# Nine groups of the down projection: each product of 264 token columns sent as two of 132

## The chip, the cores and the metric

The kernel runs on one core of a Trainium2 chip. The metric is the device time of one execution in microseconds; two executions of the kernel before took 1300.14 and 1300.42 us, median 1300.28. The core has TensorE (matrix products), VectorE, ScalarE, GpSimd, and SyncE, which here only issues DMA transfers. In the profile PE is TensorE's stream of products and PEld its stream of weight loads.

## The reference

One inference step of a decoder layer over 256 prompt tokens and 8 single-token samples, 264 token columns in all, with a model width of 2048 and an inner width of 8192. Cut to the part that the change touches:

```python
hid = jnp.square(jax.nn.relu(rms_norm(x, g_mlp) @ w_up))   # (264, 8192)
x = x + hid @ w_down                                       # (264, 2048)
...
y_prompt = rms_norm(xp, g_final)
```

Ahead of it stand an input projection, three gated branches (pooling, a linear recurrence, a convolution) and an output projection. All data are 32-bit floats.

## The kernel before

**Layout.** Features lie on the 128 partitions and the 264 tokens along the free axis, so a product is a 128 x 128 block of weights (stationary) times 128 x 264 activations (moving) into an accumulator of 128 x 264 in one of eight PSUM banks.

**Three products per block.** For precision each operand is split into a high part, rounded to the type that TensorE takes in one pass (float32r), and the low rest. `mm3` (line 183) sends for one block `whi x xh`, `whi x xl` and `wlo x xh`, lines 185, 186 and 187, all into the same accumulator. `sent` (line 165) orders the moving columns: column 2j is token j and column 2j + 1 is token j + 132; `res` (line 172) reads the accumulator back in the order of the tokens.

**Stream of weights.** `weight_plan` (line 57) lists groups; a group makes four output tiles (512 output features) from k-tiles of 128 rows. All groups are cut into chunks of 1024 weights a partition (two k-tiles by 512 columns). SyncE's queue brings two chunks with one transfer, ScalarE rounds a chunk to `whi` (line 162), VectorE subtracts to `wlo` (line 163), each three chunks ahead of TensorE, in four buffers.

**The loop.** The loop over `chunks` (line 916) is the order of all engines, written out by hand. For a chunk of a group, `tile_mm` (line 901) is called for 2 k-tiles x 4 output tiles. With the last chunk of a group its four accumulators are evacuated, and the next group goes on in the other four banks.

**The MLP.** It runs in four quarters q of the inner width: four groups `w_up`, then four groups `w_down` (m = 0 to 3, 16 k-tiles from k0 = 16 q). The activations of a quarter are in `A` (q even) or in `LH` and `Q` (q odd), by `hid` (line 798). `down_evac` (line 824) adds an accumulator to the residual `X` (line 830); in the fourth quarter it also starts the final norm, whose sums are products with a constant tile `ones` (line 980). The down projection has 16 groups of 8 chunks; a group has 8 x 2 x 4 x 3 = 192 products.

```python
mm3(pss[m], whi[:, i % NHI, s], wlo[:, i % NHI, s], xh, xl, c == 0 and kt == 0 and gi > 2, stop)
```

Of the kernel before, what the change touches and what calls it, by code (L numbers as in the profile page):

```python
# [13 lines left out]
ALU = mybir.AluOpType  # L14
# [6 lines left out]
N = TP + TS  # L21
# [26 lines left out]
NHI = 4  # L48
# [8 lines left out]
def weight_plan():  # L57

    groups = [("w_lru_in", 0, 2 * WIDE, 0)] + [("w_in", WIDE, KD - WIDE, m) for m in (1, 2)]
    groups += [("w_in", 0, 16, m) for m in (0, 3, 4, 6, 5)]
    for g in range(4):
        groups += [("w_gate", 0, 16, t) for t in ((0, 4, 1), (5,), (2, 6), (3, 7))[g]]
        groups += [("w_pool_br", 0, 4, g), ("w_lru_br", 0, 8, g)]
    groups += [("w_gate", 0, 16, 8 + g) for g in range(3)]
    groups += [("w_conf_br", 0, 4, 0), ("w_gate", 0, 16, 11)]
    groups += [("w_conf_br", 0, 4, g) for g in range(1, 4)]
    groups += [("w_out", 0, 16, m) for m in range(4)]
    for q in range(4):  # L70
        groups += [("w_up", 0, 16, q * 4 + m) for m in range(4)]
        groups += [("w_down", q * 16, 16, m) for m in range(4)]
    chunks = []
    for gi, (name, _, k, m) in enumerate(groups):
        for c in range(k // 2):
            chunks.append(("wide" if name == "w_lru_in" else "dense", gi, c, CH))
            if name == "w_in" and (m, c) in LRU_AT:
                chunks.append(("lru", LRU_AT.index((m, c)), 0, 512))
            if (name, m) == ("w_gate", 0) and c == 3:
                chunks += [("grp", 0, 0, 512), ("none", 0, 0, 0)]  # L80
    return groups, chunks
# [3 lines left out]
def hybrid_step(ctx: ExitStack, tc: tile.TileContext, head_in, x_in, par_in, st_in, wall, y_out, st_out):  # L85
    nc = tc.nc
# [9 lines left out]
    whi = cpool.tile([P, NHI, CH], F32R, name="whi")  # L96
    wlo = cpool.tile([P, NHI, CH], F32R, name="wlo")
    qtmp = cpool.tile([P, 16 * N], F32, name="qtmp", tag="Q")
    first = cpool.tile([P, KD + EARLY * ROW], F32, name="first")
    early = first[:, KD:].rearrange("p (k c) -> p k c", k=EARLY)  # L100
    X = cpool.tile([P, KD, N], F32, name="X")
# [19 lines left out]
    def acc():  # L121
        return psum.tile([P, 512], F32, name="acc", tag="acc")
# [7 lines left out]
    groups, chunks = weight_plan()  # L130
# [34 lines left out]
    def sent(x):  # L165

        return x.rearrange("p (t j) -> p j t", t=2)

    def halves(x):
        return x.rearrange("p (t j) -> p t j", t=2)  # L170

    def res(ps):

        return ps[:, :N].rearrange("p (j t) -> p t j", t=2)

    def spread(prompt, sample, ps, f):

        r, h = res(ps), N // 2
        for d, a, t in ((prompt[:, :h], r[:, 0, :], slice(0, h)), (prompt[:, h:], r[:, 1, :TP - h], slice(h, TP)),
                        (sample, r[:, 1, TP - h:], slice(TP, N))):  # L180
            nc.vector.tensor_tensor(d, a, f[:, t], op=ALU.mult)

    def mm3(ps, whi_t, wlo_t, xh, xl, first, last):
        xh, xl = sent(xh), sent(xl)
        nc.tensor.matmul(ps[:, :N], whi_t, xh, start=first, stop=False)  # L185
        nc.tensor.matmul(ps[:, :N], whi_t, xl, start=False, stop=False)  # L186
        nc.tensor.matmul(ps[:, :N], wlo_t, xh, start=False, stop=last)  # L187
# [19 lines left out]
    def later(n, fn):  # L207
        delayed.append((now[0] + n, fn))
# [26 lines left out]
    def spend(**kw):  # L235
        for e, c in kw.items():
            credit[e] -= c
# [133 lines left out]
    TM, GEL, RA, _ = B  # L371
# [22 lines left out]
    def lru_x_evac(ct, ps):  # L394
        spread(el[:, ct, 3:], st_lc[:, ct, :, 3], ps, rstd)
        spend(dve=0.5)
# [165 lines left out]
    def ca_evac(ct, ps):  # L562
        spread(vext[:, ct, 30:], st_cc[:, ct, :, 30], ps, SG[:, ct, :])
        spend(dve=0.5)
# [89 lines left out]
    def pool_evac(gi, ps):  # L654
        spread(pext[:, gi, 15:], st_po[:, gi, :, 15], ps, rstd)
        spend(dve=0.5)
# [135 lines left out]
    def square_add(m, add=True):  # L792
        t = sq2 if m == 0 else G[:, 21 + m % 3, :]
        nc.scalar.activation(t, X[:, m, :], AF.Square)  # L794
        if m and add:
            nc.gpsimd.tensor_tensor(sq2, sq2, t, op=ALU.add)  # L796
# [24 lines left out]
    def half(h):  # L821
        return slice(h * (N // 2), (h + 1) * (N // 2))

    def down_evac(q, m, ps):
        if (q, m) == (3, KD - 1):
            for h in range(2):
                nc.vector.tensor_tensor(X[:, m, half(h)], X[:, m, half(h)], res(ps)[:, h, :], op=ALU.add)
                nc.vector.tensor_tensor(G[:, 11, half(h)], X[:, m, half(h)], X[:, m, half(h)], op=ALU.mult)
            return
        nc.vector.tensor_tensor(halves(X[:, m, :]), halves(X[:, m, :]), res(ps), op=ALU.add)  # L830
        spend(dve=0.4)
        if q == 3:
            def rest():
                square_add(m, m < KD - 2)
                nc.scalar.activation(X[:, m, :], X[:, m, :], AF.Copy, scale=gfin[:, m:m + 1])

            later(0 if m >= KD - 4 else 1 + m % 4 // 2, rest)


    def group(gi):  # L840
        name, k0, _, m = groups[gi]
        if name == "w_in":
            def rhs(i):
                return A[:, i, :], A[:, 16 + i, :]
            fn = {0: pool_evac, 1: lru_x_copy, 2: lambda c, p: lru_x_evac(4 + c, p), 3: gel_evac,
                  4: lambda c, p: gel_evac(4 + c, p), 5: ca_evac, 6: cb_evac}[m]
            return rhs, fn
        if name == "w_gate":
            return (lambda i: (A[:, i, :], A[:, 16 + i, :])), (lambda c, p: gate_evac(m // 4, m % 4, c, p))
        if name == "w_pool_br":  # L850
            assert "grp" in done
            return (lambda i: (Q(i), Q(8 + i))), (lambda c, p: branch_evac(0, m, c, p))
        if name == "w_lru_br":
            assert "lru" in done
            return (lambda i: (LH(i), LH(8 + i))), (lambda c, p: branch_evac(1, m, c, p))
        if name == "w_conf_br":
            assert "conf" in done
            return (lambda i: (Q(4 + i), Q(12 + i))), (lambda c, p: branch_evac(2, m, c, p))
        if name == "w_out":
            return (lambda i: (A[:, i, :], A[:, 16 + i, :])), (lambda c, p: out_evac(m * 4 + c, p))  # L860
        if name == "w_up":
            return bpart, (lambda c, p: up_evac(m // 4, (m % 4) * 4 + c, p))
        q = k0 // 16
        return (lambda i: hid(q, i)), (lambda c, p: down_evac(q, m * 4 + c, p))
# [36 lines left out]
    def tile_mm(i, gi, c, kt, m, rhs, pss, stop):  # L901
        s = slice(kt * 512 + m * P, kt * 512 + (m + 1) * P)
        xh, xl = rhs(2 * c + kt + (WIDE if gi < 3 else 0))
        mm3(pss[m], whi[:, i % NHI, s], wlo[:, i % NHI, s], xh, xl, c == 0 and kt == 0 and gi > 2, stop)


# [8 lines left out]
    pss = None  # L915
    for i, ch in enumerate(chunks):
# [17 lines left out]
        kind, gi, c, _ = ch  # L934
        if kind == "dense":
            rhs, fn = group(gi)
            n = groups[gi][2] // 2
            if c == 0:
                pss = [acc() for _ in range(4)] if gi > 2 else pair[4 * gi - 4:4 * gi]
            if i < len(chunks) - 2:  # L940
                for kt in range(2):
                    if i == 13 and kt == 1:
                        x_rms()
                    for m in range(4):
                        tile_mm(i, gi, c, kt, m, rhs, pss, c == n - 1 and kt == 1)
            elif i == len(chunks) - 1:
                for m in range(4):
                    for b in range(4):
                        tile_mm(i - 1 + b // 2, gi, c - 1 + b // 2, b % 2, m, rhs, pss, b == 3)
            if c == n - 1:  # L950
                for m in range(4):
                    fn(m, pss[m])
                after(gi)
        elif kind == "lru":
            for j in range(2):
                lru_gate_mm(2 * gi + j, i, j)
            if gi == 3:
                lru_tail()
        elif kind == "grp":
            grp_mm(i)  # L960
# [16 lines left out]
    ps = [acc(), acc()]  # L977
# [4 lines left out]
    t, last = G[:, 9, :], acc()  # L982
# [129 lines left out]
```

## Time and profile before

| | |
|---|---|
| two executions | 1300.14, 1300.42 us (median 1300.28) |
| span of the profiled execution, first to last instruction | 1299.3 us |
| mean granted TensorE clock | 0.997 |
| products, weight loads | 11434, 11434 |
| moved from and to memory | 252.03 MB read, 3.21 MB written, 196 GB/s over the span |
| last product of the down projection | starts at 1287.0 us |

The profile gives an instruction's line in the kernel, its engine, output and inputs by the program's names, and its time from the span's start. A product's record is longer than the step from one product to the next, since products are pipelined. Idle time before an instruction is put down to what released it. A line such as 187 belongs to a helper; the tiles tell which stage called it (`A` or `LH` and `Q` as the moving side are the activations of the down projection, among others).

### The profile page before, as it was taken

The page shows a single profiled execution, that of the slowest core. Times are in us where ns is not written, and L with a number is a line of the kernel's source. Part 1 is how long each engine was busy: PE and PEld are TensorE (multiplying, and loading weights), DVE is VectorE, ACT ScalarE, POOL GpSimd, SP SyncE. Part 2 cuts the span into 40 slices and gives each one's busy share as a digit, 9 for nine tenths or more (in the row PEclk, how much of TensorE's full clock was granted, in tenths as well). Part 3 has the DMA queues.
Part 4 walks back from the last instruction along what each step waited for, and adds up shares of the span by engine and source line. Part 5 has one row for each costly group of instructions (what it writes and reads, how often), then busy time and mean ns, then how long its engine had stood idle before and what let it go on. Part 6 is the DMA issues. An engine that isn't in the chain of part 4 may idle for free.

```text
span 1299.3 us, 26672 instructions
## 1 busy us (share of the span) xinstructions
PE 1287.7 (99%) x11434; PEld 1286.8 (99%) x11434; DVE 834.7 (64%) x1058; ACT 717.7 (55%) x1021; POOL 104.6 (8%) x124
## 2 busy tenths in 40 slices
PE   9999999999999999999999999999999999999996
PEld 9999999999999999999999999999999999999996
DVE  6896898776776677666655555655555555555554
ACT  7767677667674655455544334543344533354543
POOL 0250010110102023021000000000000000000013
PEclk9999999999999999999999999999999999999998
DMA  8656566555565564656555555555555555555551
GB/s 337 220 186 202 191 207 200 195 195 198 196 229 193 186 206 161 232 185 206 195 194 198 195 197 194 198 197 194 197 195 196 195 197 195 197 196 196 195 195 68
DMA packets 38711, 256.96 MB, mean 198 GB/s; under 512 B 4288, under 2 KB 5312, under 8 KB 9152
## 3 DMA queue, kind: packets, MB, share of 16 engines
q1 hardware_dynamic: 38304, 254.78, 57.8%
q8 instruction: 89, 1.46, 0.4%
q10 hardware_dynamic: 288, 0.47, 0.1%
q14 instruction: 30, 0.25, 0.1%
HBM read 252.03 MB, written 3.21 MB: 196 GB/s over the span
## 4 chain that ended last, share of the span: by engine, by line
PE 99%; DVE 0%; DMA 0%; ACT 0%; SPq 0%; DVEq 0%; issue 0%
PE acc L187 33%; PE acc L186 33%; PE acc L185 33%; PE acc L894 1%; DMA first<-head_dram 0%; DVE raw L999 0%; PE acc L980 0%; SPq L151 0%; DVE acc L993 0%; DVEq L1091 0%; DVE G L992 0%; DVE G L991 0%; ACT whi L162 0%; ACT A L284 0%; PE acc L259 0%
## 5 line engine op out<-in xcount | busy, mean ns | idle before, releaser
L163 DVE TENSOR_TENSOR wlo<-raw,whi 128x1024 fp32r<-128x1024 f32 (+1 forms) x479 | 585.6, 1225 | 442.1 <-ACT whi L162 436.5
L162 ACT CAST whi<-raw 128x1024 fp32r<-128x1024 f32 (+1 forms) x479 | 493.6, 1033 | 526.1 <-PE acc L186 474.7
L187 PE MATMUL acc<-A,wlo 128*128 128x264 f32 x1952 | 538.9, 276 | 0.0
L186 PE MATMUL acc<-A,whi 128*128 128x264 f32 x1952 | 538.8, 276 | 0.0
L185 PE MATMUL acc<-A,whi 128*128 128x264 f32 x1952 | 538.7, 276 | 0.0
L187 PEld LDWEIGHTS acc<-A,wlo 128*128 128x128 f32 x1952 | 368.9, 189 | 0.1
L185 PEld LDWEIGHTS acc<-A,whi 128*128 128x128 f32 x1952 | 368.9, 189 | 0.0
L186 PEld LDWEIGHTS acc<-A,whi 128*128 128x128 f32 x1952 | 368.9, 189 | 0.0
L186 PE MATMUL acc<-xn,whi 128*128 128x264 f32 x1024 | 282.6, 276 | 0.0
L187 PE MATMUL acc<-xn,wlo 128*128 128x264 f32 x1024 | 282.6, 276 | 0.0
L185 PE MATMUL acc<-xn,whi 128*128 128x264 f32 x1024 | 282.6, 276 | 0.0
L185 PEld LDWEIGHTS acc<-xn,whi 128*128 128x128 f32 x1024 | 193.5, 189 | 0.0
L186 PEld LDWEIGHTS acc<-xn,whi 128*128 128x128 f32 x1024 | 193.5, 189 | 0.0
L187 PEld LDWEIGHTS acc<-xn,wlo 128*128 128x128 f32 x1024 | 193.5, 189 | 0.0
L186 PE MATMUL acc<-Q,whi 128*128 128x264 f32 x644 | 177.7, 276 | 0.0
L185 PE MATMUL acc<-LH,whi 128*128 128x264 f32 x640 | 176.6, 276 | 0.0
L187 PE MATMUL acc<-LH,wlo 128*128 128x264 f32 x640 | 176.6, 276 | 0.0
L186 PEld LDWEIGHTS acc<-Q,whi 128*128 128x128 f32 x644 | 121.7, 189 | 0.0
L185 PEld LDWEIGHTS acc<-LH,whi 128*128 128x128 f32 x640 | 121.0, 189 | 0.0
L187 PEld LDWEIGHTS acc<-LH,wlo 128*128 128x128 f32 x640 | 121.0, 189 | 0.0
L796 POOL TENSOR_TENSOR G<-G 128x264 f32<-128x264 f32 x28 | 25.5, 911 | 745.3 <-ACT G L794 744.4
L576 ACT ACTIVATE G<-tmp,par 128x256 f32<-128x256 f32 x120 | 54.2, 499 | 2.9 <-DVE G L579 2.0
(186 smaller groups left out, 797.3 us busy)
## 6 DMA issues: line engine op xcount, KB each, us to landing
raw<-wall_dram SPq DMA_DIRECT2D x230, 1024.0 KB, 4.9
raw<-wall_dram SPq DMA_DIRECT2D x10, 512.0 KB, 7.0
raw<-wall_dram SPq DMA_DIRECT2D x5, 256.0 KB, 3.0
X<-x_dram SPq DMA_DIRECT2D x4, 264.0 KB, 8.5
so_dram<-st SPq DMA_DIRECT2D x1, 1018.0 KB, 9.1
st<-st_dram SPq DMA_DIRECT2D x1, 912.0 KB, 9.8
y_dram<-raw SPq DMA_DIRECT2D x4, 198.0 KB, 2.2
X<-x_dram SPq DMA_DIRECT2D x1, 528.0 KB, 9.9
```

The lines of the kernel that those rows point to most:

```text
L162: nc.scalar.copy(h[:, s], r)
L163: nc.vector.tensor_tensor(lo[:, s], r, f(h[:, s]), op=ALU.subtract)
L185: nc.tensor.matmul(ps[:, :N], whi_t, xh, start=first, stop=False)
L186: nc.tensor.matmul(ps[:, :N], whi_t, xl, start=False, stop=False)
L187: nc.tensor.matmul(ps[:, :N], wlo_t, xh, start=False, stop=last)
L576: nc.scalar.activation(dst[:, ct, :TP], vext[:, ct, k:k + TP], AF.Copy, scale=par[:, w:w + 1])
L796: nc.gpsimd.tensor_tensor(sq2, sq2, t, op=ALU.add)
L894: nc.tensor.matmul(pair[m][:, :N], w[:, m * P:(m + 1) * P], sent(A[:, x, :]), start=start and k == 0, stop=False)
```

## The change

The three quarters k0 = 0, 16, 32 of the down projection, groups m = 0, 1, 2, go through a new helper `mm6`: each product of 264 columns becomes two of 132, with the same weights, into the two halves of the same accumulator. `form_of` picks the way in which the tokens are cut in two: m = 0 "far" (a half is 66 tokens from the first half of the tokens and 66 from the second, taken in turn), m = 1 "near" (a half is 132 neighbouring tokens, taken in turn from its own two halves), m = 2 "row" (132 neighbouring tokens in order). In the quarters k0 = 0 and 16 the two halves of a product follow each other; in k0 = 32 (`by_half`) the three products of one half come first, then the three of the other. The evacuation reads the accumulator back in the order of the form. Only the first of the six starts an accumulator. The groups m = 3, the fourth quarter and all else are as before.

```diff
@@ -179,6 +179,42 @@
         for d, a, t in ((prompt[:, :h], r[:, 0, :], slice(0, h)), (prompt[:, h:], r[:, 1, :TP - h], slice(h, TP)),
                         (sample, r[:, 1, TP - h:], slice(TP, N))):
             nc.vector.tensor_tensor(d, a, f[:, t], op=ALU.mult)
+
+    def quarter(x, form, s):
+        if form == "far":
+            return x.rearrange("p (t s j) -> p s j t", t=2, s=2)[:, s]
+        if form == "near":
+            return x.rearrange("p (s t j) -> p s j t", t=2, s=2)[:, s]
+        return x.rearrange("p (s j) -> p s j", s=2)[:, s]
+
+    def back(ps, form):
+        if form == "far":
+            return ps[:, :N].rearrange("p (s j t) -> p t s j", t=2, s=2)
+        if form == "near":
+            return ps[:, :N].rearrange("p (s j t) -> p s t j", t=2, s=2)
+        return ps[:, :N].rearrange("p (s j) -> p s j", s=2)
+
+    def like(x, form):
+        if form == "far":
+            return x.rearrange("p (t s j) -> p t s j", t=2, s=2)
+        if form == "near":
+            return x.rearrange("p (s t j) -> p s t j", t=2, s=2)
+        return x.rearrange("p (s j) -> p s j", s=2)
+
+    def form_of(gi):
+        name, k0, _, m = groups[gi]
+        if name != "w_down" or k0 > 32 or m == 3:
+            return None, False
+        return ("far", "near", "row")[m], k0 == 32
+
+    def mm6(ps, whi_t, wlo_t, xh, xl, first, last, form, by_half):
+        todo = [(w, x, s) for w, x in ((whi_t, xh), (whi_t, xl), (wlo_t, xh)) for s in range(2)]
+        if by_half:
+            todo = todo[0::2] + todo[1::2]
+        n = N // 2
+        for i, (w, x, s) in enumerate(todo):
+            nc.tensor.matmul(ps[:, s * n:(s + 1) * n], w, quarter(x, form, s), start=first and i == 0,
+                             stop=last and i == 5, skip_group_check=True)
 
     def mm3(ps, whi_t, wlo_t, xh, xl, first, last):
         xh, xl = sent(xh), sent(xl)
@@ -827,7 +863,11 @@
                 nc.vector.tensor_tensor(X[:, m, half(h)], X[:, m, half(h)], res(ps)[:, h, :], op=ALU.add)
                 nc.vector.tensor_tensor(G[:, 11, half(h)], X[:, m, half(h)], X[:, m, half(h)], op=ALU.mult)
             return
-        nc.vector.tensor_tensor(halves(X[:, m, :]), halves(X[:, m, :]), res(ps), op=ALU.add)
+        form = form_of(len(groups) - 32 + 8 * q + 4 + m // 4)[0]
+        if form:
+            nc.vector.tensor_tensor(like(X[:, m, :], form), like(X[:, m, :], form), back(ps, form), op=ALU.add)
+        else:
+            nc.vector.tensor_tensor(halves(X[:, m, :]), halves(X[:, m, :]), res(ps), op=ALU.add)
         spend(dve=0.4)
         if q == 3:
             def rest():
@@ -901,6 +941,10 @@
     def tile_mm(i, gi, c, kt, m, rhs, pss, stop):
         s = slice(kt * 512 + m * P, kt * 512 + (m + 1) * P)
         xh, xl = rhs(2 * c + kt + (WIDE if gi < 3 else 0))
+        form, by_half = form_of(gi)
+        if form:
+            mm6(pss[m], whi[:, i % NHI, s], wlo[:, i % NHI, s], xh, xl, c == 0 and kt == 0, stop, form, by_half)
+            return
         mm3(pss[m], whi[:, i % NHI, s], wlo[:, i % NHI, s], xh, xl, c == 0 and kt == 0 and gi > 2, stop)
```

## The prediction

> **What bounds the kernel now.** I read the page first, for the engine that sets the end. The rows are busy time and instructions by engine, the granted clock in 40 slices, and the chain of waits by engine.
>
> ```profile
> span 1299.3 us, 26672 instructions
> ...
> PE 1287.7 (99%) x11434; PEld 1286.8 (99%) x11434; DVE 834.7 (64%) x1058; ACT 717.7 (55%) x1021; POOL 104.6 (8%) x124
> ...
> PEclk9999999999999999999999999999999999999998
> ...
> PE 99%; DVE 0%; DMA 0%; ACT 0%; SPq 0%; DVEq 0%; issue 0%
> ...
> L186 PE MATMUL acc<-A,whi 128*128 128x264 f32 x1952 | 538.8, 276 | 0.0
> ...
> L186 PEld LDWEIGHTS acc<-A,whi 128*128 128x128 f32 x1952 | 368.9, 189 | 0.0
> ```
>
> TensorE is the whole chain, at full clock. There are as many weight loads as products: line 186, which uses the same weights as line 185 just before it, has 1952 loads of its own for its 1952 products. So a product carries a load whether or not the weights are new.
>
> Next I read the timeline of TensorE where the change acts. I show the first and the last of 57 consecutive product starts, then a few products with their loads (start, length, engine):
>
> ```profile
> 999.81 0.28 PE L187 MATMUL acc<-xn,wlo 128*128 128x264 f32 x1
> ...
> 1006.11 0.28 PE L186 MATMUL acc<-xn,whi 128*128 128x264 f32 x1
> ```
> ```profile
> 699.88 0.28 PE L185 MATMUL acc<-A,whi 128*128 128x264 f32 x1
> 699.88 0.19 PEld L186 LDWEIGHTS acc<-A,whi 128*128 128x128 f32 x1
> 700.00 0.28 PE L186 MATMUL acc<-A,whi 128*128 128x264 f32 x1
> 700.00 0.19 PEld L187 LDWEIGHTS acc<-A,wlo 128*128 128x128 f32 x1
> 700.11 0.28 PE L187 MATMUL acc<-A,wlo 128*128 128x264 f32 x1
> ```
>
> 56 steps in 6.30 us are 112.5 ns for one product. The records are longer (276 and 189 ns) because they hold pipeline latency; the pace, not the record, is the price. The load for the next product starts with the current product (699.88 and 699.88, 700.00 and 700.00): one load is in flight ahead, no more. A load that is shorter than the 112.5 ns in which the current product streams costs nothing. How much shorter it is decides this change, and the busy stream hides it.
>
> So I looked for loads that nothing covers. The kernel's last products (line 980) give one: they stop for VectorE, and the stream begins anew at 1288.54. The first two rows give min, median and max in ns over all of that line; then come the first load alone, two loads, two products:
>
> ```profile
> L980 PEld LDWEIGHTS acc<-G,ones x12: 186/190/190, 1287.0 to 1288.6; 128*128 128x128 f32 x12
> L980 PE MATMUL acc<-G,ones x12: 276/276/380, 1287.1 to 1288.8; 128*128 128x132 f32 x12
> ```
> ```profile
> 1288.54 0.19 PEld L980 LDWEIGHTS acc<-G,ones 128*128 128x128 f32 x1 [0.24 <-DVE G L828]
> ...
> 1288.54 0.30 PEld L980 LDWEIGHTS acc<-G,ones 128*128 128x128 f32 x2 [0.24 <-DVE G L828]
> ...
> 1288.54 0.49 PE L980 MATMUL acc<-G,ones 128*128 128x132 f32 x2
> ```
>
> The first product there takes 380 ns in place of 276: it waits 104 ns for its weights. The second load starts 0.30 - 0.19 = 0.11 us after the first. So a 128 x 128 load of four-byte weights keeps its path for 104 to 110 ns. Today it fits under 112.5 ns with a few nanoseconds to spare.
>
> **The change, part by part.** The nine groups are quarters 0 to 2 of the down projection with m = 0, 1, 2. A group has 8 chunks, each of 2 k-tiles, 4 column tiles and 3 products: 192 products, 192 x 0.1125 = 21.6 us, and 9 x 192 = 1728 products, 194.4 us of the span. The windows of two of these groups show that nothing but TensorE fills them:
>
> ```profile
> 682.00:703.60 21.60, 21.60 (x195) 21.60 (x194) 12.54 (x18) 11.31 (x16) 0.00 (x0) 1.00 0.59 199
> 725.20:746.80 21.60, 21.60 (x195) 21.60 (x194) 11.17 (x14) 8.37 (x8) 0.00 (x0) 1.00 0.59 193
> ```
>
> (Span, then busy us of PE, PEld, VectorE, ScalarE, GpSimd, the clock, the DMA share, GB/s.)
>
> Removed: 1728 products of 264 columns, 194.4 us, all on the path. Added: 3456 products of 132 columns, all on the path, each with its own load of 128 weights, since a load is part of every product here. A half has half the columns, so its stream needs about 112.5 / 2 = 56 ns; its successor's load needs 104 to 110 ns and can only start when the half starts. The later of the two decides, and that is the load. No row shows a four-byte product of 132 columns at the one-pass rate, so I bound its pace: 104 ns below (the exposed wait), 112.5 ns above (the pace that such loads keep without delaying anything). I take 108.5 ns, by the row that is nearest, two loads 0.11 us apart with no stream ahead of them.
>
> 3456 x 0.1085 = 375.0 us, less 194.4 us: **180.6 us more**. The ends: 3456 x 0.104 - 194.4 = +165.0; 3456 x 0.1125 - 194.4 = +194.4, a doubling of the nine groups.
>
> The three ways of choosing the halves (far, near, row) and the order by halves in the third quarter change which columns a half reads and whether neighbours share weights. Under a bound by loads neither counts: the load reads weights, not tokens, and line 186 loads weights that line 185 has just loaded. I take nothing for them. On the reading side a step through memory is free already: the 264 columns of lines 185 to 187 come from two places 132 apart, at 112.5 ns, and the contiguous columns of line 980 keep the same pace for the same load, six products in (0.84 - 0.28) / 5 = 0.112 us each.
>
> ```profile
> 1287.13 0.84 PE L980 MATMUL acc<-G,ones 128*128 128x132 f32 x6
> ```
>
> The rest hides. The 36 evacuations read and write X in the order of the halves; the same 128 x 264 elements move by VectorE in one instruction each, four after a group:
>
> ```profile
> 703.54 1.44 DVE L830 TENSOR_TENSOR X<-X,acc 128x264 f32<-128x264 f32 x4
> ```
> ```profile
> ACT whi L162 <- PE acc L186: 223.3, 135, 1.7
> DVE wlo L163 <- ACT whi L162: 185.1, 134, 1.5
> ```
>
> 1.44 us stand against 21.6 us until those four of the eight accumulators are needed again, so even three times that costs nothing; without that cover it would be at most 9 x 1.44 = 13 us. The waits (first all from 682 to 1093 us, in total, count and longest) show ScalarE's split waiting for TensorE and VectorE for ScalarE, not the other way: with TensorE slower both wait longer and are still there in time. The DMA queue follows VectorE in turn. Instructions come no faster than now: one product each 108.5 ns in place of 112.5. No wait is added, and the tail after the last group (line 980 on) isn't touched, as the fourth quarter stays whole.
>
> The profiled execution has a span of 1299.3 us; the two runs have a median of 1300.28, 1.0 us above it. That 1.0 us stays: 1299.3 + 1.0 + 180.6 = **1480.9, say 1481 us**; by the ends 1465 to 1495.
>
> **The rivals.** *The load hides under the half* (not slower). The only slow-clock restart speaks for it, at 4.07 us, before the clock is up: a load alone, two loads, and the durations over the line.
>
> ```profile
> 4.07 0.29 PEld L894 LDWEIGHTS acc<-A,whi 128*128 128x128 f32 x1 [0.21 <-ACT whi L162]
> ...
> 4.07 0.47 PEld L894 LDWEIGHTS acc<-A,whi 128*128 128x128 f32 x2 [0.21 <-ACT whi L162]
> ...
> L894 PEld LDWEIGHTS acc<-A,whi x64: 186/189/305, 4.1 to 15.4; 128*128 128x128 f32 x64
> ```
>
> If the second of these is the 305 ns one, it starts 0.47 - 0.305 = 0.165 us after the first: at half the clock 1.5 times the 0.11, not twice. That fits a fixed 55 ns and 55 ns that go by the clock. If the fixed part can run under the product ahead, a load takes 55 ns of its path and a half 56: the change costs nothing, **1300 us**. It decides once a load's own share is below 56 ns. Against it: at 1288.54 the second load waited 0.11 us although nothing streamed, so it waited for the first load whole, fixed part and all, and in the stream a load starts only with the product ahead. Chance 0.07. By the Trainium skill, page "TensorE: Matmul & The Clock Gate", section "Wait — 56ns, not 53.3ns?", each product at full clock pays some 2.5 ns beside its columns; then this rival would give 4.3 us more.
>
> *The load hides in part.* Midway between 56 and 108.5 a half takes 82 ns: 1728 x (0.164 - 0.1125) = +89 us, **1389 us**. The restart rows speak against it as above; for it speaks that they are a restart, not a stream. Chance 0.08. The same page, section "Back-to-back issue gap", has about 81 ns as the sustained pace of load and product pairs of 128 columns; by that, an estimate of +86 us, where the trace's restarts show 104 to 110 ns for these loads.
>
> *Short products take the slow path of four-byte data.* Line 980 has plain four-byte operands: 6 products of 132 columns are 12 records at 112.5 ns, so 225 ns for each. If a half of 132 columns is run like this: 1728 x (0.450 - 0.1125) = +583 us, **1883 us**. For it: it is the only 132-column row there is. Against it: the operands of the halves keep the type that does 264 columns in one pass. Chance 0.05.
>
> *The clock falls*, since half-empty products leave the array idle for half the time. Then a load takes the 0.165 us of the slow restart: 3456 x 0.165 - 194.4 = +376 us, **1676 us**. The slices of the clock show full speed through all stretches, but in none is the array half idle. Chance 0.02.
>
> **How the numbers follow.** The forecast (each half pays its own load) has 0.77, the four rivals 0.07, 0.08, 0.05 and 0.02. The predicted time is 1481. The forecast's own range, 1465 to 1495, falls just short of 8 in 10; taken down to the half-hidden load and up a little for what sits around the stream, 1388 to 1500 us, it holds 0.77 + 0.08 = 0.85. Two per cent are 26 us, about what can be told from no change. Faster by more than that: a product can't stream its columns in less than it does, and nothing else on the path goes; 0.01. Within 2%: the hidden load, 0.07. Slower: 0.92.
>
> **What would show it.** Right: in the nine groups product starts are 108 to 109 ns apart, load starts the same, some 13,160 products in all, each changed group lasts about 41.7 us, the clock stays full, VectorE's and ScalarE's busy time stays, their waits for TensorE grow. Far, near and row alike, and the order by halves no different. Wrong: starts 56 to 58 ns apart (hidden load), two in a row 57 and then 108 (a load saved where neighbours share weights), 220 ns or twice the records (slow path), a clock below 1, or groups that differ by form, which would mean that the reading of tokens has a price after all. It would also be wrong if an evacuation grew so long that TensorE waits at the head of a group.

## The result, and the profile after

Two executions of the changed kernel took 1491.88 and 1492.34 us, median 1492.11, against 1300.28 before: a ratio of 1.1475, 95% interval 1.1442 to 1.1508. The change makes the kernel 191.8 us slower. The profiled execution's span is 1490.1 us, 190.8 us longer.

The page after, in the parts that were read before:

```profile
span 1490.1 us, 30128 instructions
...
PE 1478.8 (99%) x13162; PEld 1477.9 (99%) x13162; DVE 837.7 (56%) x1058; ACT 717.9 (48%) x1021; POOL 104.8 (7%) x124
...
PEclk9999999999999999999999999999999999999999
...
PE 99%; DVE 0%; DMA 0%; ACT 0%; DVEq 0%; issue 0%
PE acc L216 26%; PE acc L221 24%; PE acc L222 24%; PE acc L223 24%; PE acc L934 1%; DVE raw L1043 0%; DMA first<-head_dram 0%; PE acc L1024 0%; DVE acc L1037 0%; DVEq L1135 0%; DVE G L1036 0%; DVE G L1035 0%; PE acc L295 0%; ACT whi L162 0%
...
L216 PE MATMUL acc<-A,whi 128*128 128x132 f32 x1536 | 245.7, 275 | 0.0
L216 PEld LDWEIGHTS acc<-A,whi 128*128 128x128 f32 x1536 | 217.6, 192 | 0.0
```

TensorE is still the whole chain at full clock. It has 13162 products and 13162 loads: 1728 more of each. The new helper's line 216 alone is 26% of the chain. VectorE's and ScalarE's busy times moved by 3.0 us and 0.2 us.

Where in the nine groups the time went shows in the last evacuation of each group (timeline of VectorE, start and length; the line has moved to 868). The first three rows end a far, a near and a row group of the first quarter. The last two end a far and a near group of the third quarter, where the order goes by halves:

```profile
724.68 0.43 DVE L868 TENSOR_TENSOR X<-X,acc 128x264 f32<-128x264 f32 x1 [0.24 <-PE acc L216]
...
767.56 0.43 DVE L868 TENSOR_TENSOR X<-X,acc 128x264 f32<-128x264 f32 x1 [0.24 <-PE acc L216]
...
810.45 0.43 DVE L868 TENSOR_TENSOR X<-X,acc 128x264 f32<-128x264 f32 x1 [0.24 <-PE acc L216]
...
1197.96 0.43 DVE L868 TENSOR_TENSOR X<-X,acc 128x264 f32<-128x264 f32 x1 [0.24 <-PE acc L216]
...
1240.84 0.43 DVE L868 TENSOR_TENSOR X<-X,acc 128x264 f32<-128x264 f32 x1 [0.24 <-PE acc L216]
```

From end to end a near group takes 42.88 us, a row group 42.89, a near group by halves 42.88; before, a group took 21.6. That is 384 halves at 111.67 ns. Neither the form nor the order by halves, in which fewer neighbours share weights, moves it. The loads keep the beat themselves, first in a far group (the second and the last of 57 such rows), then in a near group (of 60), two rows being six loads apart.

```profile
684.67 0.30 PEld L216 LDWEIGHTS acc<-A,wlo 128*128 128x128 f32 x2
...
721.52 0.30 PEld L216 LDWEIGHTS acc<-A,wlo 128*128 128x128 f32 x2
...
726.88 0.30 PEld L216 LDWEIGHTS acc<-A,wlo 128*128 128x128 f32 x2
...
765.74 0.30 PEld L216 LDWEIGHTS acc<-A,wlo 128*128 128x128 f32 x2
```

55 steps of six loads in 36.85 us and 58 in 38.86 us are both 111.67 ns a load. 3456 x 0.11167 = 385.9 us, less the 194.4 us of before, is 191.5 us: the whole loss. TensorE waits for nobody in the changed groups. The waits of the other engines grew: ScalarE's for TensorE (in total, count and longest, over the whole run) stood in one row before and stand in two rows after.

```profile
ACT whi L162 <- PE acc L186: 474.7, 307, 2.4
...
ACT whi L162 <- PE acc L222: 372.8, 244, 3.4
ACT whi L162 <- PE acc L216: 275.1, 66, 4.3
```

### The profile page after: what moved, and what is told of

It is laid out like the page before. It is cut to its first block, busy times and chain, and to the rows that moved or that the text cites. A ratio compares the mean times of both kernels' runs of the same rounds, so it can differ in the third digit from the quotient of the medians.

```text
span 1490.1 us, 30128 instructions
## 1 busy us (share of the span) xinstructions
PE 1478.8 (99%) x13162; PEld 1477.9 (99%) x13162; DVE 837.7 (56%) x1058; ACT 717.9 (48%) x1021; POOL 104.8 (7%) x124
## 4 chain that ended last, share of the span: by engine, by line
PE 99%; DVE 0%; DMA 0%; ACT 0%; DVEq 0%; issue 0%
PE acc L216 26%; PE acc L221 24%; PE acc L222 24%; PE acc L223 24%; PE acc L934 1%; DVE raw L1043 0%; DMA first<-head_dram 0%; PE acc L1024 0%; DVE acc L1037 0%; DVEq L1135 0%; DVE G L1036 0%; DVE G L1035 0%; PE acc L295 0%; ACT whi L162 0%; ACT rstd L1030 0%
## 5 line engine op out<-in xcount | busy, mean ns | idle before, releaser
L221 PE MATMUL acc<-A,whi 128*128 128x264 f32 x1568 | 432.9, 276 | 0.0
L222 PE MATMUL acc<-A,whi 128*128 128x264 f32 x1568 | 432.8, 276 | 0.0
L223 PE MATMUL acc<-A,wlo 128*128 128x264 f32 x1568 | 432.8, 276 | 0.0
L221 PEld LDWEIGHTS acc<-A,whi 128*128 128x128 f32 x1568 | 296.4, 189 | 0.0
L222 PEld LDWEIGHTS acc<-A,whi 128*128 128x128 f32 x1568 | 296.4, 189 | 0.0
L223 PEld LDWEIGHTS acc<-A,wlo 128*128 128x128 f32 x1568 | 296.3, 189 | 0.0
L216 PE MATMUL acc<-A,whi 128*128 128x132 f32 x1536 | 245.7, 275 | 0.0
L216 PEld LDWEIGHTS acc<-A,whi 128*128 128x128 f32 x1536 | 217.6, 192 | 0.0
L216 PE MATMUL acc<-A,wlo 128*128 128x132 f32 x768 | 179.8, 275 | 0.0
L216 PEld LDWEIGHTS acc<-A,wlo 128*128 128x128 f32 x768 | 132.1, 192 | 0.0
L222 PE MATMUL acc<-Q,whi 128*128 128x264 f32 x452 | 124.8, 276 | 0.0
L221 PE MATMUL acc<-LH,whi 128*128 128x264 f32 x448 | 123.7, 276 | 0.0
L223 PE MATMUL acc<-LH,wlo 128*128 128x264 f32 x448 | 123.6, 276 | 0.0
```

What stands on the lines that cost most here:

```text
L216: nc.tensor.matmul(ps[:, s * n:(s + 1) * n], w, quarter(x, form, s), start=first and i == 0, stop=last and i == 5, skip_group_check=True)
```

## The experiments

Three theories can give 111.7 ns for a half. **Load:** each product carries a load of 128 columns of four-byte weights, and no product can follow another faster than its load. **Short product:** a product with few columns has a fixed price, whatever its weights. **Serial:** the load of a half waits until the half ahead has streamed, 55 ns and then 57 ns; for it speaks that in the changed kernel a load starts 0.06 us before its product's record, where it led by 0.11 us before. All edits are in the nine groups and, where not said otherwise, against the changed kernel. Each time is compared with runs of the kernel before on the same chip.

### Eight columns in place of two halves

```diff
-        for i, (w, x, s) in enumerate(todo):
-            nc.tensor.matmul(ps[:, s * n:(s + 1) * n], w, quarter(x, form, s), ...
+        for i, (w, x) in enumerate(((whi_t, xh), (whi_t, xl), (wlo_t, xh))):
+            nc.tensor.matmul(ps[:, :8], w, x[:, :8], start=first and i == 0, stop=last and i == 2, ...
```

> Each of the 1728 products of the nine groups is sent once, for 8 token columns instead of 264; the other 256 columns are left out, and the evacuation adds 8 columns. Load theory (a product can't be sent faster than its own weight load, 111.7 ns, however few columns it has): the nine groups stay at 192 x 0.1117 = 21.4 us each and the time is 1300.3 - 1728 x 0.0008 = 1298.9 us. Serial theory (the load runs only after the product ahead has streamed: 55 ns of stream and 57 ns of load make the 112): 8 columns stream in 3 ns, the pace is 60 ns, 1300.3 - 1728 x 0.0525 = 1209.6 us. Short-product theory (a fixed price of 111.7 ns for a product with few columns, whatever its weights): 1298.9 us, as the load theory.

Measured: 1471.78 us against 1300.69, ratio 1.1316 (1.13 to 1.1331). None of the three said so. Ninety-seven parts in 100 of the token columns are gone, and the kernel is 171 us slower than with all of them. The granted clock tells why. Windows of this run inside a changed group and in an unchanged stretch (the column after the engines is the clock), then the second and the second-last of 47 rows three products apart:

```profile
700.00:760.00 60.00, 60.00 (x283) 60.00 (x283) 15.68 (x18) 11.69 (x12) 0.00 (x0) 0.50 0.31 105
850.00:900.00 50.00, 50.00 (x447) 50.00 (x446) 29.10 (x39) 27.45 (x41) 0.00 (x0) 1.00 0.58 193
```
```profile
725.87 0.35 PE L212 MATMUL acc<-A,wlo 128*128 128x8 f32 x1
...
754.03 0.35 PE L212 MATMUL acc<-A,wlo 128*128 128x8 f32 x1
```

44 steps of three products in 28.16 us are 213.3 ns a product: with the array almost idle the clock went to half, and the load took 1.9 times the 111.67 ns. A price of 213 ns for 8 columns is no price by columns, and the serial theory's 60 ns, or twice that at half clock, is not what was measured. What the load costs at full clock, without the fall, was left to the run with 110 columns below.

### Weights of half the width, and of three quarters

```diff
-            nc.tensor.matmul(ps[:, s * n:(s + 1) * n], w, quarter(x, form, s), ...
+            nc.tensor.matmul(ps[:64, s * n:(s + 1) * n], w[:, :64], quarter(x, form, s), ...
```

> The 3456 halves of the changed kernel with 64 weight columns in place of 128: half of the output features of the nine groups are left out. Load theory, load in proportion to its weight columns: 56 to 59 ns, about as long as the 132 columns stream, so 1300.3 + 1728 x (0.112 to 0.118 - 0.1125) = 1300 to 1310 us. Short-product theory: 1492 us. Serial theory: 55 + 28 = 83 ns a half, 1393 us. If a load has a large fixed part (55 of 110 ns), 83 to 85 ns a half, about 1395 us.

Measured: 1312.23 us against 1300.69, ratio 1.0089 (1.0076 to 1.0103). 3456 halves, as many as in the changed kernel and as short, are nearly free once their loads are half as wide. That ends the short-product and the serial theory. The shorter lead of the loads then reads otherwise: in the changed kernel a half's record (min, median, max over a line) is 275 ns long, 54 more than the shortest, the first of a group. The reading that fits is that a half is issued early and waits for its weights inside its record.

```profile
L216 PE MATMUL acc<-A,whi x1536: 221/275/280, 681.7 to 1283.3; 128*128 128x132 f32 x192
```

With 64 weight columns, the near groups' pace (second and second-last of 44 rows, six halves apart):

```profile
706.08 0.28 PE L216 MATMUL acc<-A,wlo 128*64 128x132 f32 x2
...
720.43 0.28 PE L216 MATMUL acc<-A,wlo 128*64 128x132 f32 x2
```

41 steps of six in 14.35 us are 58.3 ns. The row groups took 62.0 ns by the same reading, which is enough for the 2 us above the expected range; it is taken up with the orders below.

With 96 weight columns (`ps[:96]`, `w[:, :96]`):

> The 3456 halves of the changed kernel with 96 weight columns in place of 128; a quarter of the output features of the nine groups is left out. Load theory with the size found so far (64 columns 58.3 ns, 128 columns 111.7 ns, so 0.833 ns a column and 5 ns): 85 ns a half, 16.3 us more a group than 16.3, each group 32.6 us, the time 1300.3 + 1728 x (0.170 - 0.1125) = 1399.7 us, in all three forms alike. If a load went in steps (64 or 128 columns): 111.7 ns, 1492 us, or 58.3 ns, 1307 us.

Measured: 1400.22 us against 1300.96, ratio 1.0763 (1.0745 to 1.0781). The four evacuations at the end of a near group and those at the end of the row group after it begin 32.65 us apart, 85.0 ns a half (before, a group took 21.6 us, so it is 11.0 us longer, not the 16.3 of the expectation, whose total uses the right figure):

```profile
745.84 1.96 DVE L868 TENSOR_TENSOR X<-X,acc 96x264 f32<-96x264 f32 x4 [0.42 <-PE acc L216]
778.49 1.95 DVE L868 TENSOR_TENSOR X<-X,acc 96x264 f32<-96x264 f32 x4 [0.42 <-PE acc L216]
```

58.3, 85.0 and 111.67 ns for 64, 96 and 128 columns lie on one line: 0.833 ns a weight column and 5 ns for each load. The 64-column point stands only 2 ns above the 56 ns of a half's stream; that the load sets it too rests on its lying on the line of the other two.

### One product of 110 columns, and of 88

As with eight columns, but for the first 55 (or 44) pairs of the usual order:

```diff
+            nc.tensor.matmul(ps[:, :110], w, sent(x)[:, :55], start=first and i == 0, stop=last and i == 2, ...
```

> The same with 110 token columns, 46 ns of 111.7 ns, 41 parts in 100; the other 154 columns are left out. If the clock holds: 1298.9 us; if it falls: about 1472 us. The changed kernel's halves, 55 of 111.7 ns, held it.

Measured: 1299.45 us against 1300.81, ratio 0.999 (0.998 to 0.9999). With 154 of 264 columns left out the kernel is 1.4 us faster, as the load's 111.67 ns against 112.5 ns said. Second and last of 63 rows, three products apart: 61 steps in 20.43 us, 111.6 ns a product. Narrower weights had also made the output smaller; here the output shrinks with the tokens, and the price stays that of 128 weight columns.

```profile
704.36 0.28 PE L212 MATMUL acc<-A,wlo 128*128 128x110 f32 x1
...
724.79 0.28 PE L212 MATMUL acc<-A,wlo 128*128 128x110 f32 x1
```

> As with 8 columns, but each of the 1728 products is sent once for 88 token columns; the other 176 are left out. 88 columns stream in 37 ns of a load's 111.7 ns, a third of the time. If the clock holds: 111.7 ns a product, 1298.9 us. If it falls as with 8 columns and with quarters of 66 (a quarter of the time): up to 213.3 ns, about 1472 us.

Measured: 1467.93 us against 1300.81, ratio 1.1283 (1.1264 to 1.1301). Fewer columns than in the run with 110, and 168 us more: the clock fell, as with eight. The first window is of the run with 110 columns, the second of the run with 88:

```profile
704.00:725.00 21.00, 21.00 (x190) 21.00 (x190) 10.33 (x14) 8.26 (x8) 0.00 (x0) 1.00 0.56 189
...
720.00:760.00 40.00, 40.00 (x190) 40.00 (x189) 10.58 (x14) 7.99 (x8) 0.00 (x0) 0.50 0.31 105
```

At 112.5 ns for 264 columns, 110 columns stream for 47 of 111.67 ns, 42 parts in 100 of the time, and 88 columns for 34. So the clock holds at 42 and falls at 34; the changed kernel's halves have 50.

### Quarters

```diff
+        todo = [(w, x, s) for w, x in ((whi_t, xh), (whi_t, xl), (wlo_t, xh)) for s in range(4)]
+        n = N // 4
...
+            nc.tensor.matmul(ps[:, s * n:(s + 1) * n], w, sent(x)[:, s * 33:(s + 1) * 33], ...
```

> Each product of the nine groups as four of 66 columns, in the order of the kernel before: the suspected cost doubled. Load theory at full clock: 4 x 111.7 = 446.7 ns a product, 1300.3 + 1728 x (0.4467 - 0.1125) = 1877.8 us. If the clock falls as with 8 columns (the array streams for a quarter of the time here, for half of it in the changed kernel, for 3 parts in 100 with 8 columns): 4 x 213.3 ns, up to 2580 us. If short products had a price by columns instead: 2 x 111.7 ns as with halves, 1492 us.

Measured: 2573.81 us against 1300.96, ratio 1.9789 (1.976 to 1.9819). The loads of the nine groups take twice as long for their number and nearly twice again by the clock. The first window is the head of the first changed group, the second lies inside the second one:

```profile
682.00:685.00 3.00, 3.00 (x30) 3.00 (x29) 2.45 (x5) 2.52 (x5) 0.00 (x0) 1.00 0.45 191
900.00:1000.00 100.00, 100.00 (x471) 100.00 (x470) 6.55 (x6) 5.22 (x5) 0.00 (x0) 0.50 0.06 22
```

471 products in 100 us are one each 212 ns. PE reads as fully busy in both.

### The orders alone

Whole products of 264 columns, read far, near or row, and written to the accumulator in order in all three:

```diff
+            nc.tensor.matmul(ps[:, :N], w, whole(x, form), start=first and i == 0, stop=last and i == 2)
```

> The far, near and row orders alone: the nine groups send their tokens in these orders, but each product whole, 264 columns at once, and evacuate as the changed kernel does. All theories in which the order of the tokens is free: 112.5 ns a product, 1300.3 us, within 0.5 us. If reading in one of the orders costs something by itself, that form's three groups are longer than 21.6 us.

Measured: 1306.1 us against 1300.69, ratio 1.0043 (1.003 to 1.0055). The expectation of a free order failed, and by one form. The near rows first (second and second-last of 45), then the row form's (of 41):

```profile
706.26 0.28 PE L219 MATMUL acc<-A,wlo 128*128 128x264 f32 x1
...
720.45 0.28 PE L219 MATMUL acc<-A,wlo 128*128 128x264 f32 x1
...
728.43 0.28 PE L219 MATMUL acc<-A,wlo 128*128 128x264 f32 x1
...
742.31 0.28 PE L219 MATMUL acc<-A,wlo 128*128 128x264 f32 x1
```

Near: 42 steps of three in 14.19 us, 112.6 ns. Row: 38 steps in 13.88 us, 121.8 ns. Tokens read side by side cost 9 ns a product more than tokens taken in turn from two places. In the changed kernel this hides: 61 ns a half lie under 111.67.

Does the price come of meeting the load, which reads memory at the same time? The row order in all nine groups, with weights of half the width (`ps[:64]`, `w[:, :64]`):

> Whole products of 264 columns in the row order in all nine groups, with 64 weight columns in place of 128 (half of the output features left out): is the price of the row order (121.5 to 122 ns a product where 112.5 was expected) one of reading tokens side by side, or of meeting the weight load on its way? Reading alone: 121.5 to 122 ns, 1300.3 + 1728 x 0.0092 = 1316 us. Meeting the load, whose reads are halved: about 117 ns, 1308 us.

Measured: 1314.99 us against 1300.96, ratio 1.0108 (1.0093 to 1.0123); 14.0 us in 1728 products are 8.1 ns each. Halving the load's reads takes away about 1 of the 9 ns. Most of the price is one of the reading itself; what makes it was not found.

### Two-byte operands

```diff
+            nc.tensor.matmul(ps[:, s * n:(s + 1) * n], top(w), quarter(top(x), form, s), ...
```

`top` views every second two-byte element, the upper half of each value.

> The 3456 halves of the changed kernel as they are, but weights and tokens of the nine groups are read as the upper two bytes of each value (bf16), so the low bytes are left out of these groups. Load theory: loads of two-byte weights stood 32 ns apart at the kernel's start, so a load is no longer the bound; the pace is that of 132 columns, 56 to 57.5 ns, and the time 1300 to 1305 us. Short-product theory: still 111.7 ns a half, 1492 us. Serial theory: 55 ns of stream and up to 32 ns of load, 87 ns a half, 1300.3 + 1728 x 0.0615 = 1407 us.

Measured: 1477.75 us against 1300.69, ratio 1.1362 (1.1345 to 1.138), which no theory had. The forms part widely. Rows six halves apart: far (second and second-last of 47), near (of 53), row (of 51).

```profile
690.79 0.45 PE L219 MATMUL acc<-A,wlo 128*128 128x132 bf16 x2
...
728.47 0.45 PE L219 MATMUL acc<-A,wlo 128*128 128x132 bf16 x2
...
740.56 0.40 PE L219 MATMUL acc<-A,wlo 128*128 128x132 bf16 x2
...
776.57 0.40 PE L219 MATMUL acc<-A,wlo 128*128 128x132 bf16 x2
...
785.33 0.28 PE L219 MATMUL acc<-A,wlo 128*128 128x132 bf16 x2
...
802.60 0.28 PE L219 MATMUL acc<-A,wlo 128*128 128x132 bf16 x2
```

44 steps in 37.68 us are 142.7 ns a half, 50 in 36.01 us 120.0, 48 in 17.27 us 60.0. The row groups come within 3 ns of what the load theory says: two-byte loads bind no more. The other two have a price of their own, so the whole run tests the theory only in its row third. Whether that price belongs to the columns or to the load:

> Whole products of 264 columns in the three orders with the upper two bytes alone (bf16), low bytes left out of the nine groups: are the 142.7 ns (far) and 120 ns (near) of a bf16 half a price of the token columns, or of the load? By the columns: 285, 240 and at most 122 ns a product, 1300.3 + 576 x (0.1725 + 0.1275 + 0.005) = 1476 us. By the load, once for each product: 142.7, 120 and 112.5 ns, 1300.3 + 576 x (0.0302 + 0.0075) = 1322 us.

Measured: 1471.64 us against 1300.96, ratio 1.1312 (1.1295 to 1.1329): by the columns. It is the reading of two-byte tokens in turn from two places, about 1.06 ns a column far and 0.9 near, that is slow; the four-byte type has it the other way round.

No run points to a version that is faster than the kernel before: its products stream 112.5 ns, and the load leaves no less than 111.67.

## Why the prediction was right

The forecast was that each half pays its own load: 1481 us, range 1388 to 1500. It is 1492.1.

**The bound.** That a load belongs to every product and hides under 112.5 ns with little to spare was right, and the runs with 64 and 96 weight columns and with 110 token columns show it from both sides: fewer weights made the halves cheap, fewer tokens saved 1.4 us.

**The price of a load** is the term that was mis-sized. Taken was 108.5 ns, "by the row that is nearest, two loads 0.11 us apart with no stream ahead of them"; it is 111.67 ns. 3456 x 0.00317 = 11.0 us, the gap between 1480.9 and 1492.1 up to 0.2 us. The 104 to 110 ns of the restart are near 128 x 0.833 = 106.7 ns, the columns alone, so it seems that the restart lacks most of the 5 ns which each load has beside them in a steady stream; no run shows that by itself. The upper end, the pace that loads keep, was the nearer row. The ends 1465 to 1495 held it.

**Shared weights.** Right: a half with the weights of the half before pays a full load, and the order by halves changes nothing (42.88 us both ways).

**The orders.** Taken at nothing, and nothing they cost here, but for a reason that was half wrong. "The contiguous columns of line 980 keep the same pace" argued from plain four-byte products, where 132 columns take the 112 ns that 264 take in the type of the halves; at half the speed a price of reading need not show. The trace of before had the right row, the four products of line 259, whose tokens lie side by side in the one-pass type:

```profile
L259 PE MATMUL acc<-parts,ones_r x4: 284/284/287, 41.9 to 606.6; 128*128 128x264 f32 x4
```

284 ns where the others have 276: most of the 9 ns of the row order stood there. That the nothing came true is in this part luck: the price is covered only because the load is longer.

**What hides.** Evacuations, splits and transfers stayed off the path: an evacuation went from 0.423 to 0.429 us, and TensorE's waits in the whole run are two, of 0.8 and 0.2 us, both in its first microseconds.

**The rivals.** *The load hides* rested on a fixed part of 55 ns drawn from the one restart at half clock. The widths say 5 ns, so nothing that size can slip under the stream. *Hides in part*: a part that hides would be missing from every width alike, and the line through the three has 5 ns added and nothing taken off. *Slow path*: there are 13162 records, not twice as many for a half, and a half with narrower weights takes 58.3 ns. *The clock falls* was given 0.02 and did not happen, but this was closer than that: with the array streaming a third of the time it does happen, with 42 parts in 100 not. The price put on it, 1676 us, was too low; at half clock a load takes 213.3 ns, not 165, so by an estimate 3456 halves would have given 1300.3 + 3456 x 0.2133 - 194.4 = 1843 us.

## What to carry to other kernels

Compare a product's stream with its own weight load before cutting it: with four-byte weights a load takes 0.833 ns a weight column and 5 ns, 111.7 ns for 128, so 264 token columns just cover it and fewer save next to nothing. Look for loads that nothing covers in the trace, but take their price from the steady stream rather than from a restart: the shortest pace that is known to hide them (112.5 ns here) is an upper bound, and here the nearer one. And watch the granted clock where loads outweigh the stream: cutting again, into quarters, doubled the number of loads and then halved the clock.

## What had not been expected of the hardware

The clock fell to half although PE read as busy all the time: with 8, 66 and 88 columns to a load of 111.67 ns (the array streams 3, 25 and 34 parts in 100 of the time) it fell, 3 to 4 us after the first changed product; with 110 and 132 (42 and 50) it held. The far two-byte halves, 132 columns every 142.7 ns (39 by the same count), kept it at 1.00 too; whether a slow read counts as streaming no run shows. The rows of busy time show none of this, only the granted clock does. At half clock a load takes 213.3 ns, twice the 106.7 ns of the columns alone, so the 5 ns do not show there. The Trainium skill, page "TensorE: Matmul & The Clock Gate", section "What's actually happening", has the clock follow how busy the array has recently been, in windows of about 3.4 us; the 3 to 4 us from the first changed product to the fall agree, with the addition that weight loads under way do not count as enough.

Reading order matters, and by type in opposite ways. Four-byte tokens side by side take 121.8 ns for 264 columns, in turn from two places 112.5 to 112.6; two-byte tokens at every second place take 117 ns side by side, 237 and 280 in turn. The last three are from the run with whole two-byte products, rows three products apart; here the far form (second and second-last of 48, 45 steps, 37.80 us):

```profile
691.09 0.44 PE L222 MATMUL acc<-A,wlo 128*128 128x264 bf16 x1
...
728.89 0.44 PE L222 MATMUL acc<-A,wlo 128*128 128x264 bf16 x1
```

The Trainium skill, page "SBUF — State Buffer", section "Door 1: The DMA port swizzle", has neighbours in one 16-byte line read at full speed and each new line at a price. The two-byte runs fit that in direction, though it does not tell far from near; the four-byte runs contradict it, and the measurement decides.
